# Adding the later rows in PSUM with VectorE, and draining the pipeline after each tile, in a prefix log-sum-exp kernel

## The chip, the cores and the metric

The kernel runs on one core of a Trainium2 chip. The metric is device time in microseconds (us), the median of several executions. Five engines work side by side: TensorE (PE, with its weight loads PEld), VectorE (DVE), ScalarE (ACT), GpSimd (POOL) and SyncE (SP), which here only issues DMA transfers.

## The reference, cut to what matters

```python
B, S, D = (4, 4096, 4128)
out[:, 0, :] = x[:, 0, :]
for t in range(1, S):
    mx = np.maximum(out[:, t - 1, :], x[:, t, :])
    out[:, t, :] = mx + np.log(np.exp(out[:, t - 1, :] - mx) + np.exp(x[:, t, :] - mx))
```

It is a running log-sum-exp along the sequence. The kernel takes exp of everything, makes a prefix sum and takes Ln.

## The kernel before

A tile is 128 x r consecutive rows of the sequence, r of them in each partition (r is 3 in 40 tiles and 2 in 4). It is worked in four chunks of 1024 columns; the last 32 columns, the **tail**, go with chunk 3. Each chunk has a head on TensorE: triangular matrices sum the exponentials over partitions, and `pick` adds the carry of the tile before.

```python
def head(self):                     # 2 matmuls of 512 columns for each line
    ...
    for j in range(t.r):
        for s in range(0, CH, MM):
            mm(pt[:, s:s + MM], excl if j else incl, self.e(j, s, s + MM), start=j == 0)
    if not t.first:
        for s in range(0, CH, MM):
            mm(pt[:, s:s + MM], pick, carry[self.c][:, s:s + MM])
    ...

def stage(self, j):
    t, c, pt = self.t, self.c, self.pt
    nc.scalar.activation(t.xt[:, j, c * CH:(c + 1) * CH], pt, ACT.Ln)
    if j + 1 < t.r:
        for s in range(0, CH, MM):
            mm(pt[:, s:s + MM], ident, self.e(j + 1, s, s + MM), stop=j + 2 == t.r)
        if c == last and j == 0:
            nc.scalar.activation(t.xt[:, :, t0:D], self.qt, ACT.Ln)    # the tail, all rows
            keep(carry_t, self.qt[:, t.r - 1, :])
    else:
        keep(carry[c], pt)          # two VectorE instructions: the carry copy
```

After Ln of row j, an identity matmul adds row j + 1's exponentials in PSUM. PSUM has three buffers for chunks (`pt`) and two for tails (`qt`). The loop runs over the chunks of all tiles without a break, so one tile's last rows are finished while the next tile's exponentials begin. SBUF holds four tiles. When a tile is done, its store and the load three tiles ahead are issued.

The softmax here doesn't subtract the row's maximum and nothing guards it: scores larger than these inputs give would overflow.

## Time and profile before

| | before |
|---|---|
| time | 1262.75 us (1262.73 to 1262.77, 3 runs) |
| span of the profile | 1261.0 us |
| busy: ACT, PE, DVE | 75%, 55%, 36% |
| transfers | 541 MB, 429 GB/s, DMA row full |
| exp's wait for loads | 247.8 us |

The reading is in the prediction: its first fences show that the DMA row has no gap, that ScalarE waits for loads, and that a tile whose load is ready takes 22.73 us, while the transfers allow one every 29.25 us.

### The profile page before, as it was taken

Reading aid. Unit: us, or ns where it says so; the run is one execution under the profiler, and the core shown is the slowest. Engines: PE = TensorE matmul, PEld = TensorE weight load, DVE = VectorE, ACT = ScalarE, POOL = GpSimd, SP = SyncE. Lnnn points to the kernel's source line nnn. Section 1 sums busy time; section 2 is a strip of 40 time slices with the busy share of each in tenths; the row PEclk is TensorE's granted clock in tenths of the full one; section 3 lists DMA queues with packets and bytes.
Section 4 is the critical chain, followed back from the end, with each engine's and each line's share of the span. In section 5 each row is a group of like instructions: output and inputs, shape, how many; then the busy total and the mean of one; then the engine's idle time right before and its main releaser. Section 6 shows DMA issues by size and latency. Waiting matters only on the chain.

```text
span 1261.0 us, 6165 instructions
## 1 busy us (share of the span) xinstructions
PE 688.7 (55%) x2268; PEld 237.0 (19%) x2268; DVE 451.4 (36%) x445; ACT 947.3 (75%) x733; POOL 2.2 (0%) x13
## 2 busy tenths in 40 slices
PE   3665554555555555655346555555634755664552
PEld 1222111111121111211112211111211211221120
DVE  2443333333333333334424333333442433333344
ACT  5997777777777777778569777777966977777794
POOL 0000000000000000000000000000000000000000
PEclk9887777777677777777768777787777777778786
DMA  9999999999999999999999999999999999999998
GB/s 411 410 439 431 432 427 434 438 430 432 433 437 431 432 432 436 432 427 436 431 433 436 437 429 431 436 436 432 430 434 435 432 431 432 434 435 431 433 422 347
DMA packets 12702, 541.46 MB, mean 429 GB/s; under 512 B 1408, under 2 KB 1408, under 8 KB 1408
## 3 DMA queue, kind: packets, MB, share of 16 engines
q1 hardware_dynamic: 12672, 541.07, 99.4%
q8 instruction: 18, 0.29, 0.1%
q14 instruction: 12, 0.10, 0.0%
HBM read 270.53 MB, written 270.53 MB: 429 GB/s over the span
## 4 chain that ended last, share of the span: by engine, by line
DMA 69%; ACT 21%; PE 5%; issue 2%; DVE 1%; SPq 0%; ACTq 0%
DMA xt<-in_x_dram 67%; ACT xt L128 11%; ACT xt L162 10%; PE pt L88 5%; DMA out_dram<-xt 2%; ACT xt L167 0%; SPq L116 0%; DVE carry L92 0%; DVE carry L93 0%; ACTq L231 0%; SPq L113 0%; ACTq L128 0%; PE qt L88 0%
## 5 line engine op out<-in xcount | busy, mean ns | idle before, releaser
L128 ACT ACTIVATE xt<-xt 128x3072 f16<-128x3072 f32 (+3 forms) x176 | 478.5, 2719 | 247.9 <-DMA xt<-in_x_dram 247.8
L88 PE MATMUL pt<-xt,ident 128*128 128x512 f16 x672 | 251.3, 470 | 530.7 <-ACT xt L162 530.4
L162 ACT ACTIVATE xt<-pt 128x1024 f32<-128x1024 f32 x512 | 487.6, 1030 | 2.5 <-PE pt L88 0.7
L92 DVE CAST carry<-pt 32x1024 f16<-32x1024 f32 x176 | 216.4, 1230 | 761.0 <-ACT xt L162 760.7
L88 PE MATMUL pt<-xt,excl 128*128 128x512 f16 x672 | 247.0, 504 | 0.0
L93 DVE TENSOR_TENSOR carry<-pt,carry 32x1024 f16<-32x1024 f32 x176 | 215.9, 1227 | 6.1
L88 PEld LDWEIGHTS <-ident 128*128 128x128 f16 x672 | 70.1, 104 | 677.7 <-issue 654.0
L88 PE MATMUL pt<-xt,incl 128*128 128x512 f16 x352 | 152.0, 526 | 23.6 <-ACT xt L128 15.0
L88 PEld LDWEIGHTS <-excl 128*128 128x128 f16 x756 | 92.5, 124 | 141.0 <-issue 108.1
L88 PE MATMUL pt<-carry,pick 128*128 128x512 f16 x320 | 109.8, 429 | 0.0
L88 PEld LDWEIGHTS <-incl 128*128 128x128 f16 x480 | 45.2, 111 | 129.7 <-DVE carry L93 95.2
L88 PEld LDWEIGHTS <-pick 128*128 128x128 f16 x360 | 40.6, 113 | 57.0 <-issue 34.3
L167 ACT ACTIVATE xt<-qt 128x96 f32<-128x96 f32 (+1 forms) x44 | 10.9, 249 | 45.7 <-PE pt L88 45.7
L92 DVE CAST carry_t<-qt 32x32 f16<-32x32 f32 x44 | 8.7, 197 | 25.5 <-ACT xt L167 25.4
L88 PE MATMUL qt<-xt,incl 128*128 128x64 f16 (+2 forms) x128 | 12.3, 196 | 0.0
L88 PE MATMUL qt<-xt,excl 128*128 128x64 f16 (+1 forms) x84 | 10.6, 187 | 0.0
L93 DVE TENSOR_TENSOR carry_t<-qt,carry_t 32x32 f16<-32x32 f32 x44 | 8.5, 193 | 1.5
L88 PE MATMUL qt<-carry_t,pick 128*128 128x96 f16 (+1 forms) x40 | 8.2, 204 | 0.0
L83 DVE MEMSET carry<- 128x512 uint32 x4 | 1.9, 485 | 1.1 <-PEq L220 1.0
L70 ACT ACT_TABLE_LOAD x1 | 1.3, 1283 | 0.8 <-PEq L220 0.8
L35 POOL TENSOR_SCALAR_AFFINE_SELECT pick<-pick 128x128 f16<-128x128 f16 x2 | 0.6, 294 | 0.1
L25 POOL TENSOR_SCALAR_AFFINE_SELECT incl<-incl 128x128 f16<-128x128 f16 x1 | 0.3, 294 | 0.0
(11 smaller groups left out, 1.9 us busy)
## 6 DMA issues: line engine op xcount, KB each, us to landing
xt<-in_x_dram SPq DMA_DIRECT2D x40, 6192.0 KB, 42.2
out_dram<-xt SPq DMA_DIRECT2D x40, 6192.0 KB, 28.1
xt<-in_x_dram SPq DMA_DIRECT2D x4, 4128.0 KB, 37.3
out_dram<-xt SPq DMA_DIRECT2D x4, 4128.0 KB, 23.0
```

What stands on the lines that cost most here:

```text
L25: nc.gpsimd.affine_select(out=t, in_=t, pattern=[[1, P]], compare_op=mybir.AluOpType.is_ge, fill=0.0, base=base, channel_multiplier=-1,)
L35: nc.gpsimd.affine_select(out=t, in_=t, pattern=[[step, P]], compare_op=mybir.AluOpType.not_equal, fill=1.0, base=base, channel_multiplier=1,)
L70: nc.scalar.preload_act_table_set("natural_log_exp_and_others")
L83: nc.vector.memset(t, 0.0)
L88: nc.tensor.matmul(pt, lhsT=w, rhs=rhs, start=start, stop=stop, skip_group_check=True)
L92: nc.vector.tensor_copy(cr[HI:HI + 32, :], pt[HI:HI + 32])
L93: nc.vector.tensor_tensor(out=cr[LO:LO + 32, :], in0=pt[HI:HI + 32], in1=cr[HI:HI + 32, :], op=mybir.AluOpType.subtract,)
L128: nc.scalar.activation(self.t.half[:, :, 2 * c0:2 * c0 + w], self.t.xt[:, :, c0:c0 + w], ACT.Exp,)
L162: nc.scalar.activation(t.xt[:, j, c * CH:(c + 1) * CH], pt, ACT.Ln)
L167: nc.scalar.activation(t.xt[:, :, t0:D], self.qt, ACT.Ln)
```

## The change

The intent is to take the identity matmuls off TensorE, to let VectorE make the later rows, to keep the carry copies from delaying those adds where no head waits for a copy, and to handle each tile by itself. The core of the diff:

```diff
         def tail_head(self):
...
             for i in range(r):
-                e = self.e(i, CH, CH + tail)
-                mm(qt[:, i:, :], incl, to(e, r - i), start=i == 0)
-                if i:
-                    mm(qt[:, :i, :], excl, to(e, i))
+                mm(qt[:, 0, :], excl if i else incl, e[i], start=i == 0)
...
+            for i in range(1, r):
+                add(qt[:, i, :], qt[:, i - 1, :], e[i])

         def stage(self, j):
...
-            if j + 1 < t.r:
-                for s in range(0, CH, MM):
-                    mm(pt[:, s:s + MM], ident, self.e(j + 1, s, s + MM), stop=j + 2 == t.r)
-                if c == last and j == 0:
-                    nc.scalar.activation(t.xt[:, :, t0:D], self.qt, ACT.Ln)
-                    keep(carry_t, self.qt[:, t.r - 1, :])
-            else:
-                keep(carry[c], pt)
+            if c == last and j == 0:
+                nc.scalar.activation(t.xt[:, :, t0:D], self.qt, ACT.Ln)
+
+        def next_row(self, j):
+            add(self.pt, self.pt, self.e(j + 1, 0, CH))
...
+    for n, s in enumerate(steps):
+        chunks = [Chunk(s, c) for c in range(n_main)]
...
+        for g in range(n_main + s.r - 1):
+            at = [(chunks[g - d], d) for d in range(s.r - 1, -1, -1) if 0 <= g - d < n_main]
+            for k, d in at:
+                k.stage(d)
...
+            done += [k for k, d in at if d + 1 == s.r]
+            if g + 1 < n_main:
+                while done:
+                    done.pop(0).keep()
+            for k, d in at:
+                if d + 1 < s.r:
+                    k.next_row(d)
...
+        for k in done:
+            k.keep()
```

More of the change, by code (lines that the diff above doesn't have):

```diff
@@ L29, in tri, with ones_at @@
         return t
-    def ones_where_zero(bases, step, name):
+    def ones_at(rows, name):
         t = pool.tile([P, P], FP16, name=name)
         nc.gpsimd.memset(t, 0.0)
-        for base in bases:
+        for row in rows:
             nc.gpsimd.affine_select(
-                out=t, in_=t, pattern=[[step, P]], compare_op=mybir.AluOpType.not_equal,
-                fill=1.0, base=base, channel_multiplier=1,
+                out=t, in_=t, pattern=[[0, P]], compare_op=mybir.AluOpType.not_equal,
+                fill=1.0, base=-row, channel_multiplier=1,
             )
@@ L43, in _constants @@
         tri(-1, "excl"),
-        ones_where_zero([0], -1, "ident"),
-        ones_where_zero([-(HI + 31), -(LO + 31)], 0, "pick"),
+        ones_at([HI + 31, LO + 31], "pick"),
     )
@@ L71 @@
     consts = ctx.enter_context(tc.tile_pool(name="consts", bufs=1))
-    incl, excl, ident, pick = _constants(nc, consts)
+    incl, excl, pick = _constants(nc, consts)
     bufs = 4
@@ L85, with mm, add @@
     ctx.enter_context(tc.manual_schedule())
-    def mm(pt, w, rhs, start=False, stop=False):
-        nc.tensor.matmul(pt, lhsT=w, rhs=rhs, start=start, stop=stop, skip_group_check=True)
+    def mm(pt, w, rhs, start=False):
+        nc.tensor.matmul(pt, lhsT=w, rhs=rhs, start=start, stop=False, skip_group_check=True)
+    def add(o, a, v):
+        nc.vector.tensor_tensor(out=o, in0=a, in1=v, op=mybir.AluOpType.add)
     def keep(cr, pt):
@@ L149, in tail_head, with keep @@
             qt = self.qt = full[:, :r, :]
-            to = lambda v, n: v.unsqueeze(1).to_broadcast([P, n, tail])
+            e = [self.e(i, CH, CH + tail) for i in range(r)]
             for i in range(r):
-                e = self.e(i, CH, CH + tail)
-                mm(qt[:, i:, :], incl, to(e, r - i), start=i == 0)
-                if i:
-                    mm(qt[:, :i, :], excl, to(e, i))
+                mm(qt[:, 0, :], excl if i else incl, e[i], start=i == 0)
             if not t.first:
-                mm(qt, pick, to(carry_t, r))
+                mm(qt[:, 0, :], pick, carry_t)
+            for i in range(1, r):
+                add(qt[:, i, :], qt[:, i - 1, :], e[i])
         def stage(self, j):
-            t, c, pt = self.t, self.c, self.pt
-            nc.scalar.activation(t.xt[:, j, c * CH:(c + 1) * CH], pt, ACT.Ln)
-            if j + 1 < t.r:
-                for s in range(0, CH, MM):
-                    mm(pt[:, s:s + MM], ident, self.e(j + 1, s, s + MM), stop=j + 2 == t.r)
-                if c == last and j == 0:
-                    nc.scalar.activation(t.xt[:, :, t0:D], self.qt, ACT.Ln)
-                    keep(carry_t, self.qt[:, t.r - 1, :])
-            else:
-                keep(carry[c], pt)
+            t, c = self.t, self.c
+            nc.scalar.activation(t.xt[:, j, c * CH:(c + 1) * CH], self.pt, ACT.Ln)
+            if c == last and j == 0:
+                nc.scalar.activation(t.xt[:, :, t0:D], self.qt, ACT.Ln)
+        def next_row(self, j):
+            add(self.pt, self.pt, self.e(j + 1, 0, CH))
+        def keep(self):
+            keep(carry[self.c], self.pt)
+            if self.c == last:
+                keep(carry_t, self.qt[:, self.t.r - 1, :])
     steps = []
@@ L182 @@
         assert row == S
-    chunks = [Chunk(s, c) for s in steps for c in range(n_main)]
     ahead = bufs - 1
@@ L187 @@
         s.load()
-    stored = 0
-    chunks[0].exp()
-    chunks[1].exp()
-    chunks[0].head()
-    for g in range(len(chunks) + R - 1):
-        for d in range(R - 1, -1, -1):
-            if 0 <= g - d < len(chunks) and d < chunks[g - d].t.r:
-                k = chunks[g - d]
-                k.stage(d)
-                if k.c == last and d + 1 == k.t.r:
-                    k.t.store()
-                    if stored + ahead < len(steps):
-                        steps[stored + ahead].load()
-                    stored += 1
-        if g + 2 < len(chunks):
-            chunks[g + 2].exp()
-        if g + 1 < len(chunks):
-            chunks[g + 1].head()
+    for n, s in enumerate(steps):
+        chunks = [Chunk(s, c) for c in range(n_main)]
+        chunks[0].exp()
+        chunks[1].exp()
+        chunks[0].head()
+        done = []
+        for g in range(n_main + s.r - 1):
+            at = [(chunks[g - d], d) for d in range(s.r - 1, -1, -1) if 0 <= g - d < n_main]
+            for k, d in at:
+                k.stage(d)
+            if g == n_main + s.r - 2:
+                s.store()
+                if n + ahead < len(steps):
+                    steps[n + ahead].load()
+            done += [k for k, d in at if d + 1 == s.r]
[5 more added lines that the diff above has]
+                    k.next_row(d)
+            if g + 2 < n_main:
+                chunks[g + 2].exp()
+            if g + 1 < n_main:
+                chunks[g + 1].head()
+        for k in done:
+            k.keep()
 _INS = ['x']
```

## The prediction

> **What bounds the kernel now.** I read the page top down: busy shares first, then the slices, then the chain that ended last, then the groups, then the timeline of one tile.
>
> ```profile
> span 1261.0 us, 6165 instructions
> ...
> PE 688.7 (55%) x2268; PEld 237.0 (19%) x2268; DVE 451.4 (36%) x445; ACT 947.3 (75%) x733; POOL 2.2 (0%) x13
> ...
> DMA  9999999999999999999999999999999999999998
> ...
> DMA packets 12702, 541.46 MB, mean 429 GB/s; under 512 B 1408, under 2 KB 1408, under 8 KB 1408
> ...
> DMA 69%; ACT 21%; PE 5%; issue 2%; DVE 1%; SPq 0%; ACTq 0%
> ```
>
> No compute engine is above 75%, while the DMA row is full from the first slice to the last. Input and output are 270.5 MB each, so the floor is bytes over rate: 541 MB at some 432 GB/s is 1252 us, and the span is 1261. The chain agrees: 69% of it is DMA, nearly all of it loads. The groups say how much room the computing engines have:
>
> ```profile
> L128 ACT ACTIVATE xt<-xt 128x3072 f16<-128x3072 f32 (+3 forms) x176 | 478.5, 2719 | 247.9 <-DMA xt<-in_x_dram 247.8
> L88 PE MATMUL pt<-xt,ident 128*128 128x512 f16 x672 | 251.3, 470 | 530.7 <-ACT xt L162 530.4
> L162 ACT ACTIVATE xt<-pt 128x1024 f32<-128x1024 f32 x512 | 487.6, 1030 | 2.5 <-PE pt L88 0.7
> L92 DVE CAST carry<-pt 32x1024 f16<-32x1024 f32 x176 | 216.4, 1230 | 761.0 <-ACT xt L162 760.7
> L93 DVE TENSOR_TENSOR carry<-pt,carry 32x1024 f16<-32x1024 f32 x176 | 215.9, 1227 | 6.1
> ```
>
> ScalarE's exp waits 247.8 us for loads over 44 tiles, 5.6 us per tile. That is the room that the change may use up. The windows view shows the two regimes: one tile early in the run, when loads lay ready, and one in the steady state.
>
> ```profile
> 54.35:77.08 22.73, 15.42 (x55) 5.38 (x56) 10.21 (x10) 22.02 (x18) 0.00 (x0) 0.85 1.00 432
> 764.91:794.16 29.25, 15.36 (x54) 5.38 (x54) 10.22 (x10) 22.13 (x17) 0.00 (x0) 0.82 1.00 434
> ```
>
> The columns are window, length, then busy PE, PEld, DVE, ACT, POOL, clock, DMA share and GB/s. When loads are ready a three-row tile takes 22.73 us, with ACT busy 22.02. When they are not it takes 29.25, with DMA share 1.00 and the same ACT work. So **29.25 us per tile is the DMA period**, and computing may grow by 6.5 us per tile before it counts. The timeline of that tile:
>
> ```profile
> 764.91 2.76 ACT L128 ACTIVATE xt<-xt 128x3072 f16<-128x3072 f32 x1 [6.04 <-DMA xt<-in_x_dram]
> 767.58 2.83 ACT L162 ACTIVATE xt<-pt 128x1024 f32<-128x1024 f32 x3
> ...
> 780.75 0.34 SPq L116 DMA_DIRECT2D out_dram<-xt  x1
> 781.19 0.38 SPq L113 DMA_DIRECT2D xt<-in_x_dram  x1
> ...
> 794.16 2.76 ACT L128 ACTIVATE xt<-xt 128x3072 f16<-128x3072 f32 x1 [5.99 <-DMA xt<-in_x_dram]
> ```
>
> The store issued at 780.75 belongs to the tile before: its last rows are finished inside the next tile's work. Stores run about 15.8 us behind the next load's landing, and 13.4 us ahead of the moment when the queue would run dry (780.75 to 794.16).
>
> **What the skill says.** (1) "HBM Reference", Specifications: a core streaming alone gets about 425 GB/s, bounded by its 16 DMA engines. The trace has 429; nothing in the change touches it. (2) "VectorE: DVE Perf Modes", the TRN2 errata section: an fp32 tensor_tensor takes (N+151)/0.96 ns, 1224 for N = 1024; the subtraction at L93, with a PSUM input, measures 1227. I take 1.23 us for an add and 1.26 from start to start, as the carry pair shows (768.62 to 769.88). (3) "PSUM — Partial Sum Buffer", bank collisions: two engines must not be in one bank and quadrant together, reads included. The trace agrees: each carry copy waits for ScalarE's Ln of the same tile, though both only read. So add, Ln and copy of one chunk stay in series. (4) "TensorE: Matmul & The Clock Gate", Part 1: after an idle window of about 3.4 us the clock is halved; 512 columns then take 427 ns from start to start, and 216 when warm. The trace shows both, 0.86 and 0.43 us per pair.
>
> **The change, part by part.**
> - Removed: 672 identity matmuls (251 us of PE busy). None was on the path in steady state. A row step cost 0.68 us from Ln's end to the next Ln (1239.26 to 1239.94, warm).
> - Added: 40 three-row tiles x 8 adds + 4 two-row tiles x 4 = 336 adds x 1.23 = 413 us, and 84 tail adds x 0.2 = 17 us. DVE goes from 451 to about 880 us, 70%. A row step becomes 0.02 + 1.23 + 0.05 = 1.30 us. ScalarE's 733 instructions stay.
> - Moved: the next tile's first exp no longer overlaps the last rows, so each tile pays fill and drain. Copies of chunks 1 to 3 go after the last add and overlap the next tile's two exps.
>
> Serial time of one three-row tile, loads ready, from first exp to next first exp. Durations are from the timeline: exp 2.76 (pitch 2.67; 2.93 for the last, wider one), Ln 1.02 (pitch 0.92), a cold head of 8 matmuls 0.80 + 3 x 0.86 + 0.2 = 3.6:
> - exp 0 2.8, cold head 0 3.6 (PE idled about 9 us): first Ln at 6.45. ScalarE did exp 1 meanwhile and idles 1.1.
> - Ln, exp 2, two Ln, exp 3: 0.93 + 2.67 + 1.85 + 2.93, at 14.8. DVE's old copies end near 7.0 and its adds keep up.
> - Ln of chunk 0's last row, 15.85; its copy, 1.26 + 1.23, 18.4. Head 3 needs that PSUM buffer (three buffers, four chunks), so it starts only here; cold, 22.05. Its Ln, 23.1.
> - DVE meanwhile: two adds to 20.9, the tail adds (after head 3's tail matmuls) to 22.7, chunk 2's add to 23.96, chunk 3's first add to 25.2. Ln 26.3, add 27.55, last Ln from 27.6, next exp at **28.5 us**. With head 3 warm the same walk gives 27.8.
>
> A two-row tile gives about 22.3 the same way (20.7 for the very first, without old copies). Sum if computing alone set the pace: 13.1 first landing + 20.7 + 40 x 28.55 - 4.5 (three batch-first tiles have no carry matmuls) + 3 x 22.3 + 0.3 + 12.3 for the last store (as long as the first load of that size) + about 1 = **1252 us of span**, 1254 of time. DMA alone needs the 1261 of before. DMA stays the bound, with 0.7 us per tile to spare.
>
> Stores: a tile now ends about 28.5 us after its own landing, so the store before the next landing, not 15.8 after it; the DMA queue is fed earlier. At the end, the last tile follows 28.5 + 22.3 us after the second-last landing (1196.2): 1247, store to 1259.5; before, 1244.4 + 16.1 = 1260.5. No loss.
>
> **The rivals.**
> (a) Compute becomes the bound: fill, drain and DVE's queue exceed 29.25. For it: 0.7 us is a small margin over some twenty handoffs, and three adds lie on the last stretch. Each 0.1 us per tile beyond about 28.8 costs 4 us: 29.0 makes some 1272, 29.4 some 1288. Against: head 3 may be warm, and every duration is measured in place.
> (b) The wait just moves: row steps are slower, but ScalarE's 5.6 us of load wait shrinks to about 0.7 and the time stays 1262. This is what I expect.
> (c) Faster, since stores and loads are issued earlier. Against: the DMA row is already full, so at most the thin spots at start and end can go, a few us.
> (d) The start starves the queue, since tiles 0 and 1 no longer overlap: the second store would be issued near 62.5 where the queue lasts to about 66.8 (before, 63.44). Hidden.
>
> **Range and chances.** From (b) 1262, with a small weight of (a) on top: 1264. The low end is (c), 1258; the high end is 29.25 to 29.3 us per tile, 1284. Within 2% is 1237.5 to 1288. Over 1288 needs 0.85 us per tile more than my walk: about one in eight. Under 1237 would break the transfer floor: 0.01.
>
> **What would show it.** Right: DMA row still full; exp's wait for loads down from 247.8 to some 30 to 60 us; DVE near 880 us busy; adds near 1.23 us; tile period still 29.2; store's time to landing up from 28.1 to some 40 us or more, because it is queued earlier. Wrong: steady exps with no load wait, DMA share under 1.00 in steady windows, period above 29.3. Then the failed step would be the 28.5: an add slower into PSUM, a handoff above 0.05, or copies that hold up the first adds of the next tile.

## The result, and the profile after

The changed kernel takes **1273.52 us** (1273.11 to 1274.51, 4 runs). The kernel before, with the runs beside it, took 1262.76. The ratio is 1.0086, 95% interval 1.0069 to 1.0103: slower by 0.9%, within 2%. (A ratio is the mean time of one kernel's fast runs over that of the other's of the same rounds, so not quite the ratio of the medians.)

The page of the changed kernel (in the last three rows: line, engine and operation, output and input, count, then busy us and mean ns, then idle us just before and what ended most of it):

```profile
span 1271.1 us, 5283 instructions
...
PE 478.1 (38%) x1512; PEld 177.9 (14%) x1512; DVE 869.7 (68%) x865; ACT 978.1 (77%) x733; POOL 1.8 (0%) x11
...
DMA  9999999999999999999999999999999999999977
...
ACT 48%; DVE 26%; PE 20%; issue 4%; DMA 1%; ACTq 0%
...
L160 ACT ACTIVATE xt<-pt 128x1024 f32<-128x1024 f32 x512 | 509.3, 1023 | 267.7 <-DVE pt L89 217.2
L89 DVE TENSOR_TENSOR pt<-pt,xt 128x1024 f32<-128x1024 f32 x336 | 402.0, 1229 | 220.5 <-ACT xt L160 183.0
L129 ACT ACTIVATE xt<-xt 128x3072 f16<-128x3072 f32 (+3 forms) x176 | 475.4, 2701 | 12.5 <-DMA xt<-in_x_dram 11.1
```

The DMA row still looks nearly as full as before, and read alone it would say "bound by transfers". The chain says otherwise: DMA fell from 69% to 1%, and ACT, DVE and PE take turns. The exp row says the same. Its wait for loads is 11.1 us in all, where it was 247.8, and that is one wait, for the very first load. **Every later load lay ready when its tile began.** ScalarE now idles for VectorE instead (217.2 us before its Ln).

The timeline of one tile shows where. Columns are start, duration, engine, line, operation, output and input, and in brackets the idle time before it and what ended it:

```profile
770.66 1.06 PE L86 MATMUL pt<-carry,pick 128*128 128x512 f16 x2
...
771.79 1.02 ACT L160 ACTIVATE xt<-pt 128x1024 f32<-128x1024 f32 x1 [0.34 <-PE qt L86]
771.89 0.43 DVE L89 TENSOR_TENSOR qt<-qt,xt 128x32 f32<-128x32 f32 x2 [1.50 <-PE qt L86]
772.71 0.24 ACT L162 ACTIVATE xt<-qt 128x96 f32<-128x96 f32 x1
772.99 2.36 DVE L89 TENSOR_TENSOR pt<-pt,xt 128x1024 f32<-128x1024 f32 x2 [0.66 <-ACT xt L162]
774.25 1.02 ACT L160 ACTIVATE xt<-pt 128x1024 f32<-128x1024 f32 x1 [1.30 <-DVE pt L89]
775.44 1.02 ACT L160 ACTIVATE xt<-pt 128x1024 f32<-128x1024 f32 x1 [0.17 <-DVE pt L89]
776.50 1.23 DVE L89 TENSOR_TENSOR pt<-pt,xt 128x1024 f32<-128x1024 f32 x1 [1.15 <-ACT xt L160]
...
777.83 1.02 ACT L160 ACTIVATE xt<-pt 128x1024 f32<-128x1024 f32 x1 [1.36 <-DVE pt L89]
```

This is the drain: head 3 ends, Ln of chunk 3's first row runs, then adds and Ln alternate with nothing beside them. One line does not fit the data flow. The adds at 772.99 are for chunks 2 and 3. VectorE was free at 772.32, but waited 0.66 us for L162, Ln of the *tail*, which shares no element with them. Over the run that is 35.9 us in 44 waits, in a stretch where nothing else hides it. From the waits view (engine and line, what was waited for, total us, times, longest):

```profile
DVE pt L89 <- ACT xt L162: 35.9, 44, 2.0
```

The tile that starts at 778.75 takes 29.11 us, a hair under the transfers' 29.25. Two sums make that enough for computing to set the end. The first load lands at 13.2. The first tile takes 20.8, the other three two-row tiles 67.7 together, and 40 three-row tiles take 28.93 on average (27.82 where a batch begins, since those have no carry matmuls): the last Ln ends at 1259.1. The last store then runs alone for 12.0 us, to 1271.1. Transfers alone need the 1261 of before.

### The profile page after: what moved, and what is told of

It is laid out like the page before. It is cut to its first block, busy times and chain, and to the rows that moved or that the text cites. A ratio compares the mean times of both kernels' runs of the same rounds, so it can differ in the third digit from the quotient of the medians.

```text
span 1271.1 us, 5283 instructions
## 1 busy us (share of the span) xinstructions
PE 478.1 (38%) x1512; PEld 177.9 (14%) x1512; DVE 869.7 (68%) x865; ACT 978.1 (77%) x733; POOL 1.8 (0%) x11
## 4 chain that ended last, share of the span: by engine, by line
ACT 48%; DVE 26%; PE 20%; issue 4%; DMA 1%; ACTq 0%
ACT xt L129 27%; ACT xt L160 21%; PE pt L86 20%; DVE pt L89 14%; DVE carry L93 6%; DVE carry L94 6%; DMA xt<-in_x_dram 1%; ACT xt L162 1%; PE qt L86 0%; ACTq L160 0%; DVE carry_t L93 0%; DVE carry_t L94 0%
## 5 line engine op out<-in xcount | busy, mean ns | idle before, releaser
L160 ACT ACTIVATE xt<-pt 128x1024 f32<-128x1024 f32 x512 | 509.3, 1023 | 267.7 <-DVE pt L89 217.2
L89 DVE TENSOR_TENSOR pt<-pt,xt 128x1024 f32<-128x1024 f32 x336 | 402.0, 1229 | 220.5 <-ACT xt L160 183.0
L129 ACT ACTIVATE xt<-xt 128x3072 f16<-128x3072 f32 (+3 forms) x176 | 475.4, 2701 | 12.5 <-DMA xt<-in_x_dram 11.1
L93 DVE CAST carry<-pt 32x1024 f16<-32x1024 f32 x176 | 216.4, 1229 | 107.4 <-ACT xt L160 103.4
L86 PE MATMUL pt<-xt,excl 128*128 128x512 f16 x672 | 261.0, 527 | 0.0
L86 PE MATMUL pt<-carry,pick 128*128 128x512 f16 x320 | 129.2, 495 | 0.0
L89 DVE TENSOR_TENSOR qt<-qt,xt 128x32 f32<-128x32 f32 x84 | 16.7, 199 | 55.9 <-PE qt L86 54.5
L86 PEld LDWEIGHTS <-pick 128*128 128x128 f16 x360 | 44.0, 122 | 65.1 <-issue 47.8
L162 ACT ACTIVATE xt<-qt 128x96 f32<-128x96 f32 (+1 forms) x44 | 10.8, 245 | 0.0
L86 PE MATMUL qt<-xt,incl 128*128 128x32 f16 x44 | 9.5, 217 | 0.0
L86 PE MATMUL qt<-xt,excl 128*128 128x32 f16 x84 | 9.2, 184 | 0.0
L86 PE MATMUL qt<-carry_t,pick 128*128 128x32 f16 x40 | 7.4, 184 | 0.0
## 6 DMA issues: line engine op xcount, KB each, us to landing
out_dram<-xt SPq DMA_DIRECT2D x40, 6192.0 KB, 28.3
```

The lines of the kernel that those rows point to most:

```text
L86: nc.tensor.matmul(pt, lhsT=w, rhs=rhs, start=start, stop=False, skip_group_check=True)
L89: nc.vector.tensor_tensor(out=o, in0=a, in1=v, op=mybir.AluOpType.add)
L93: nc.vector.tensor_copy(cr[HI:HI + 32, :], pt[HI:HI + 32])
L129: nc.scalar.activation(self.t.half[:, :, 2 * c0:2 * c0 + w], self.t.xt[:, :, c0:c0 + w], ACT.Exp,)
L160: nc.scalar.activation(t.xt[:, j, c * CH:(c + 1) * CH], self.pt, ACT.Ln)
```

## The experiments

**Theory 1:** computing sets the pace of the changed kernel, and its tile is longer than I walked because chunk 2's last add waits for the tail's Ln. **Rivals:** transfers are still the bound, with gaps at start and end; or the clock of TensorE is what matters; or the adds themselves do.

The problem in testing this is that transfers hide most of a change in the computing of a tile. So most kernels below store only the first quarter of the columns, with a wrong result. That takes the transfers well below the computing and lays its pace bare:

```diff
-            nc.sync.dma_start(out=self.dram(out), in_=self.xt)
+            nc.sync.dma_start(out=self.dram(out)[:, :, :D // 4], in_=self.xt[:, :, :D // 4])
```

Each of these ran once. The state of a single run on one core is unknown, so I read from them only differences of many us and the tile periods inside their traces, which repeat within one trace.

**1. The changed kernel with quarter stores.**

> The changed kernel, but each store writes only the first quarter of the columns (wrong result on purpose), so transfers need about 18.3 us per three-row tile in place of 29.25. Theory 1 (computing sets the pace in the changed kernel): the tile period stays at 29.1 us, and the time falls only by the shorter last store, from 1273.5 to about 1266 us. Rival (transfers still set the pace, only with more gaps): the period falls well under 29 us and the time under 1150 us.

Measured: 1267.42 us, and the same tile as above:

```profile
779.73:808.84 29.11, 11.91 (x36) 4.39 (x36) 20.16 (x21) 22.89 (x18) 0.00 (x0) 0.68 0.67 273
```

The columns are window, length, busy PE, PEld, DVE, ACT and POOL, clock, DMA share and GB/s. DMA share is down to 0.67, and the length is 29.11 us to the hundredth. Computing sets the pace; the rival is out.

**2. The kernel before with quarter stores.**

> The kernel before with the same quarter stores (wrong result on purpose): its computing pace laid bare. Expected 22.73 us per three-row tile, as in the early window of its trace, and a time near 1000 us; a rival under which loads alone still hold it up would leave exp waiting for loads and a time above 1100 us.

Measured: 998.15 us and 22.73 us per tile; exp waits 13.3 us for loads in all. So the change added 6.4 us of computing to a tile, and over the whole run the transfers hide all of it but 10.8 us.

**3 and 4. The tail's Ln moved to just before the tile's last Ln, with quarter and with full stores.**

```diff
-            nc.scalar.activation(t.xt[:, j, c * CH:(c + 1) * CH], self.pt, ACT.Ln)
-            if c == last and j == 0:
-                nc.scalar.activation(t.xt[:, :, t0:D], self.qt, ACT.Ln)
+            if c == last and j + 1 == t.r:
+                nc.scalar.activation(t.xt[:, :, t0:D], self.qt, ACT.Ln)
+            nc.scalar.activation(t.xt[:, j, c * CH:(c + 1) * CH], self.pt, ACT.Ln)
```

> The changed kernel with quarter stores (wrong result on purpose) and the tail's Ln issued just before the last Ln of the tile, so that chunk 2's last add no longer comes after it. Theory 1 with the tail wait as the term that I missed: the add starts about 0.6 us earlier, the tile period goes from 29.1 to about 28.5 us and the time to some 20 us under the run of the changed kernel with quarter stores (about 1246 us). Rival (the wait is a label only, the add was held by something else): period stays 29.1 us, time within 3 us of that run.

> The same move of the tail's Ln with full stores (right result). Theory 1: computing at 28.5 us per tile falls under the DMA period of 29.25, so the time comes back to 1262 to 1265 us, ratio to the kernel before 1.000 to 1.003. Rival (the extra 10.8 us come from the start and the end, where the drained pipeline leaves the queue empty, and not from the tile period): stays at 1271 to 1274 us, ratio 1.008.

Measured: 1239.41 us with quarter stores, 28.0 less than run 1, and 28.44 us per tile. With full stores **1263.12 us** (1263.02 to 1263.43, 4 runs, right result), ratio to the kernel before 1.0004 (0.9988 to 1.0021). Moving one 0.25 us instruction takes the whole loss back. The same place in the run with quarter stores:

```profile
785.21 0.43 DVE L89 TENSOR_TENSOR qt<-qt,xt 128x32 f32<-128x32 f32 x2 [1.50 <-PE qt L86]
785.55 2.36 DVE L89 TENSOR_TENSOR pt<-pt,xt 128x1024 f32<-128x1024 f32 x2
...
789.06 1.23 DVE L89 TENSOR_TENSOR pt<-pt,xt 128x1024 f32<-128x1024 f32 x1 [1.15 <-ACT xt L162]
...
790.33 0.25 ACT L161 ACTIVATE xt<-qt 128x96 f32<-128x96 f32 x1 [1.30 <-DVE pt L89]
790.47 1.02 ACT L162 ACTIVATE xt<-pt 128x1024 f32<-128x1024 f32 x1
```

The adds follow the tail adds at once. But now the tail's Ln (L161 here) waits for chunk 3's add, although `qt` has long been ready: the tie between the two exists in both directions. With full stores the page has the signs that I had forecast for a kernel bound by transfers: exp waits 26.2 us for loads, and stores take 39.4 us to land (28.3 in the changed kernel), since they are queued earlier.

**5. The tail's Ln at its old place, one instruction per row.**

```diff
-                nc.scalar.activation(t.xt[:, :, t0:D], self.qt, ACT.Ln)
+                for i in range(t.r):
+                    nc.scalar.activation(t.xt[:, i, t0:D], self.qt[:, i, :], ACT.Ln)
```

> Quarter stores (wrong result on purpose). The tail's Ln stays at its place in the changed kernel but is cut into one instruction per row, so that its output is no longer one strided range that spans rows 0 to 2 and with them the exponentials which chunk 2's last add reads. Theory (the wait is a dependency that the framework makes out of overlapping ranges): the add no longer waits for the tail's Ln, starts about 0.6 us earlier, and the period falls to about 28.4 us, time 1236 to 1242 us. Rival (the wait belongs to the order of issue, whatever is written): the add still starts after the last of three tail Ln, period 29.1 us or more, time 1267 us or more.

Measured: 1234.71 us, 28.35 us per tile, better than the move and with 84 instructions more:

```profile
506.94 0.43 DVE L89 TENSOR_TENSOR qt<-qt,xt 128x32 f32<-128x32 f32 x2 [1.50 <-PE qt L86]
507.28 2.35 DVE L89 TENSOR_TENSOR pt<-pt,xt 128x1024 f32<-128x1024 f32 x2
507.76 0.37 ACT L163 ACTIVATE xt<-qt 128x32 f32<-128x32 f32 x3
```

The adds start before the tail's three Ln, which are still ahead of them in program order. So the wait did not belong to the order of issue. It belonged to the one instruction over all rows, and, as I read it, to the shape of its output: `xt[:, :, 4096:4128]` over three rows is one strided access whose range runs from row 0 to row 2, across the exponentials that the add reads. Written row by row there is no such range. That the framework compares whole ranges is the reading that fits every run here; I have not shown it by itself.

**6. The drain with identity matmuls in place of the large adds, quarter and full stores.**

```diff
-            add(self.pt, self.pt, self.e(j + 1, 0, CH))
+            for s in range(0, CH, MM):
+                mm(self.pt[:, s:s + MM], ident, self.e(j + 1, s, s + MM))
```

> Quarter stores (wrong result on purpose), pipeline drained per tile, but the later rows added by the identity matmuls on TensorE as before: the drain alone. My walk with a cold TensorE gives about 27.3 us per tile, so the drain costs 4.6 us of the 6.4 us between 22.7 and 29.1, and a time near 1190 us; with a warm one 25.5 us and about 1115 us. Rival (the adds are the cost, the drain is nearly free): about 24 us per tile, 1050 us.

> Full stores (right result): the drain with identity matmuls on TensorE. Its bare computing took 27.3 us per tile, under the 29.25 us of the transfers. Theory: the drain alone is hidden, 1261 to 1265 us, and exp waits for loads again. Rival (a drained pipeline costs time with any pace, through emptier queues): 1268 us or more.

Measured: 1182.17 us with quarter stores and 27.31 us per tile; with full stores 1263.23 us (one run, right result), exp waiting 83.5 us for loads. The drain costs 4.6 of the 6.4 us, and without the large adds it is hidden. The 4.6 is not the drain pure: the tail's rows are still added on VectorE, and here the identity matmuls wait for the tail's Ln, 51.9 us in 44 waits of the run with quarter stores. So up to 1.2 us of it per tile is again the tie.

**7. The adds alone, in the pipeline of the kernel before.**

```diff
-                for s in range(0, CH, MM):
-                    mm(pt[:, s:s + MM], ident, self.e(j + 1, s, s + MM), stop=j + 2 == t.r)
+                nc.vector.tensor_tensor(
+                    out=pt, in0=pt, in1=self.e(j + 1, 0, CH), op=mybir.AluOpType.add,
+                )
```

> Quarter stores (wrong result on purpose), the kernel before with its identity matmuls replaced by VectorE adds and the pipeline running on across tiles: the adds alone. VectorE then has 20.6 us of work per tile against ScalarE's 22.1, and the adds end just before the next stage needs them, so 22.7 to 23.5 us per tile and a time of 1000 to 1035 us. Rival (the adds are the cost even in a running pipeline, since copies stand ahead of them): 26 us or more, over 1120 us.

A miss: 1119.56 us and 25.3 us per tile. The waits view of this kernel names the place:

```profile
ACT xt L168 <- DVE pt L164: 136.2, 44, 3.2
```

L168 is the tail's Ln, here issued *after* the first add of chunk 3 and so held by it, 3.1 us per tile. That is the tie of run 5 once more, the other way round. So the same cut by rows was tried here:

> Quarter stores (wrong result on purpose). The adds in the running pipeline again, but with the tail's Ln cut into one instruction per row. My forecast for the adds alone (22.7 to 23.5 us) missed: 25.3 us were measured, and there the tail's Ln waited 3.1 us per tile for VectorE's adds. Theory (that wait is the same overlap of ranges as in the changed kernel, and the whole of the miss): 22.6 to 23.0 us per tile, time 995 to 1010 us. Rival (VectorE's order of copies and adds is what costs): the tile stays above 25 us and the time above 1105 us.

Measured: 988.35 us and 22.2 us per tile, under the 22.73 of the kernel before. The miss is gone, and in a running pipeline the adds cost next to nothing. That they cost nothing at all is not shown, for this kernel has one advantage over the kernel before. There too the tail's Ln (L167) waits, for the identity matmuls of chunk 3; from run 2:

```profile
ACT xt L167 <- PE pt L88: 31.2, 44, 1.1
```

These 0.7 us per tile taken off 22.73 leave some 22.0, an estimate: the kernel before was not run with its tail's Ln cut by rows. ScalarE is busy for 96% of the span of the 22.2 us kernel.

**8. Copies always ahead of the adds.**

```diff
-            if g + 1 < n_main:
-                while done:
-                    done.pop(0).keep()
+            while done:
+                done.pop(0).keep()
```

> Quarter stores (wrong result on purpose), the changed kernel with its copies always ahead of the adds: what the reordering is worth. Two pairs of copies (2.5 us each) then stand before chunk 2's and chunk 3's last adds: about 32 us per tile, a time of 1380 to 1400 us. Rival (the copies fit into gaps of VectorE, the reordering is worth nothing): within 10 us of 1267 us.

Measured: 1400.4 us and 32.4 us per tile. The order that the change chose is worth 3.3 us per tile; without it the drained kernel would have lost far more.

**9. Filler matmuls to keep TensorE's clock up.**

```diff
+            if self.c in (0, last):
+                for i in range(34 if self.c == 0 else 24):
+                    mm(fill, incl, fill_in, start=True)
             pt = self.pt = pmain.tile([P, CH], FP32, name="pt")
```

The fillers write a PSUM buffer of their own, for which the tail has one buffer in place of two.

> Quarter stores (wrong result on purpose), the changed kernel with filler matmuls into a spare PSUM bank (the tail's buffers go from two to one) ahead of the first and the last chunk's head, 34 and 24 of them, which run while TensorE would idle, so that both heads on the path run at full clock. Theory (cold heads are a part of the 29.1 us): head 0 takes 1.8 us in place of 3.6, of which 1.1 us are on the path, and head 3 gives some 0.8 more: about 27.2 us per tile, time near 1190 us, clock near 1. Rival (the clock does not matter, waits for VectorE end last): within 0.3 us of 29.1 us, or longer where fillers get in the way.

Measured: 1241.08 us, 26.3 less than run 1, so 0.66 us for each of the 40 three-row tiles in place of 1.9: the size was a miss. The mean clock rose to 0.92, but of the two heads on the path head 3 gained throughout and head 0 only in some tiles. Head 0 of two tiles, with head 3 of the second before it:

```profile
93.10 0.59 PE L90 MATMUL pt<-xt,incl 128*128 128x512 f16 x2 [3.64 <-ACT xt L133]
...
504.64 0.59 PE L90 MATMUL pt<-xt,incl 128*128 128x512 f16 x2 [1.31 <-DVE carry L98]
505.07 1.02 PE L90 MATMUL pt<-xt,excl 128*128 128x512 f16 x4
...
517.60 1.01 PE L90 MATMUL pt<-xt,incl 128*128 128x512 f16 x2 [3.64 <-ACT xt L133]
518.40 1.91 PE L90 MATMUL pt<-xt,excl 128*128 128x512 f16 x4
```

Head 3 (504.64) runs at full clock: 0.43 us from pair to next group. Head 0 at 517.60 began 3.64 us after the fillers had ended and was cold again: 0.80. The idle window of some 3.4 us that the Trainium skill states ("TensorE: Matmul & The Clock Gate", Part 1) is near that length, but this trace does not show that 3.64 us of idle time are always enough: head 0 at 93.10 came after the same 3.64 us and began at full clock. So what a warm head 0 is worth can be read here after all. From one exp of chunk 3 to the next, three-row tiles take 27.7 to 28.2 us in the 13 cases where head 0 began warm after 3.64 us, and 28.5 to 28.7 us in the 14 where it began cold (one more, where a batch begins, left out). The means differ by 0.6 us, and the shortest is 1.0 us below the cold ones, where I had expected 1.1. So cold heads are a part of the tile, as I had counted them.

Head 3 itself became 1.7 us shorter, from its first matmul to the end of its tail matmuls, but where head 0 stayed cold the tile gained only 0.4. The rest went into a longer wait for the tail's Ln, 80.7 us in all where it was 35.9:

```profile
DVE pt L93 <- ACT xt L169: 80.7, 44, 2.0
```

The tie and the cold head 3 thus cover each other. Fillers together with the cut by rows were not run.

**10. A version meant to beat both: tail by rows, and the last tile's store cut by chunk.**

```diff
             for k, d in at:
                 k.stage(d)
+                if s is steps[-1] and d + 1 == s.r:
+                    s.store_columns(k.c * CH, D if k.c == last else (k.c + 1) * CH)
             if g == n_main + s.r - 2:
-                s.store()
+                if s is not steps[-1]:
+                    s.store()
```

> Full stores (right result): the changed kernel with the tail's Ln cut by rows (28.35 us of bare computing) and the last tile's store cut into one transfer per chunk, each issued when its chunk is done, so that the queue is not empty while the last tile drains. Theory: the tile period is back at the transfers' 29.25 us, and of the last store's 12 us after the last Ln some 4 to 6 remain: 1256 to 1260 us, ratio to the kernel before 0.995 to 0.998. Rival (the end is bound by transfers already queued): 1262 to 1264 us.

Measured: 1272.23 us (1271.8 to 1272.31, 5 runs, right result), ratio 1.0073 (1.006 to 1.0087). A failure, and outside both forecasts. ScalarE in the last tile:

```profile
1233.46 1.94 ACT L163 ACTIVATE xt<-pt 128x1024 f32<-128x1024 f32 x2 [0.84 <-DVE pt L89]
1253.45 1.96 ACT L132 ACTIVATE xt<-xt 128x2112 f16<-128x2112 f32 x1 [18.05 <-DMA out_dram<-xt]
```

Until then the kernel was on time: the last tile began at 1225.10. Then exp of chunk 3 waited 18.05 us for a store to land, the only one then out for this tile, that of chunk 0. They share no column, but as ranges over two rows they overlap. I read it as the same kind of wait, this time paid at the pace of a queued transfer. Cutting that store by rows too was not tried. **No version here beats the kernel before**; the best, run 4, equals it.

## Why the prediction was right

The time, 1273.52, lies in the range, and "within 2%" had about 0.86 (one in eight and 0.01 taken off). But of my ways it was rival (a) that came true, with its own figure ("29.0 makes some 1272"), and not (b), "what I expect". That the time lies in the range is owed to its width, 1258 to 1284, and not to the mechanism: transfers as the bound, which I expected, did not hold.

- *DMA bounds the kernel before, and computing may grow by 6.5 us per tile.* Right for the first 5.7 us of it: run 2 has 22.73 us of bare computing, and the two kernels at 27.3 and 28.4 us (ident_drained and tail_late) stay within 0.5 us of 1262.75.
- *Adds of 1.23 us, DVE about 880 us.* Right: 1229 ns and 869.7 us. The 1.26 us from start to start was too much for two adds on different chunks: a pair takes 2.36, so 1.13.
- *The walk: first Ln at 6.45, 14.8 after exp 3, copy to 18.4, head 3 to 22.05, tail adds to 22.7.* Right within 0.1: in the tile from 778.75 they are 6.41, 14.82, 18.36, 22.1 and 22.7.
- *"Chunk 2's add to 23.96."* **This is the step that failed.** It starts at 23.35, not 22.73, since it waits for the tail's Ln. The shorter pair of adds gives 0.13 back and two handoffs of 0.10 in place of 0.05 take 0.1, which makes 29.11 in place of 28.5. Runs 3 and 5 take the wait away and land at 28.44 and 28.35. The prediction did name the 28.5 as the step that might fail, but for other reasons: a slower add (it took 1229 ns, as forecast) or copies that hold up the next tile's first adds (these waited for ScalarE's Ln, 0.47 us at 786.22). Only its third, handoffs above 0.05, has a small part.
- *"DMA stays the bound, with 0.7 us per tile to spare."* Wrong, and by my own numbers: the two sums, 1252 and 1261, differ by 9 us, which is 0.2 us for each of 40 tiles. First landing, two-row tiles and the last store lie outside the comparison of 28.5 with 29.25. With the measured mean of 28.93 in place of my 28.44 (28.55 less the carry matmuls' share) the sum is 1252 + 40 x 0.49 = 1272, and the span is 1271.1.
- *Exp's wait for loads at 30 to 60 us, stores at 40 us to landing.* Wrong for the changed kernel (11.1 and 28.3), as both follow from transfers being the bound.
- *Start hidden.* Right: the second store was issued at 62.95 (forecast 62.5). *No loss at the end* failed with the pace: the last store is issued at 1259.1, not 1247.

## What to carry to other kernels

When transfers hide computing, compare whole sums, with fill, short tiles and the last store in them, and not only the steady periods; and lay the pace of computing bare by shrinking the transfers before trusting a small margin. In a drained pipeline more of the handoffs lie on the path, so look there for waits between instructions that share no data. A strided output over several rows of one tile can tie together work in between; one instruction per row may be cheaper than one for all.

## What the Trainium skill lacked or had wrong

- No page that I used speaks of waits that the framework makes between accesses that share no element but whose ranges over several rows overlap, which is how I read the waits here. They cost 0.66 us per tile in the changed kernel (35.9 us in 44 waits), 3.1 us per tile with the adds in a running pipeline, and 18.05 us once where a store was cut by columns.
- "VectorE: DVE Perf Modes", the section on the DRAIN, says that an instruction that is not held starts earlier than after the full drain, but gives no amount there: two adds of 1.23 us on different PSUM buffers take 2.36 us, so the second starts 0.10 us early, while the copy pair, whose second reads the first, starts at 1.26.
- The same page's formula for an fp32 tensor_tensor is not stated for a PSUM output; here the add from PSUM to PSUM took 1229 ns, against 1224 by the formula.
